# Token-major projections with 512 columns in a matmul instead of 256

## The chip, the core and the metric

The kernel runs on one core of a Trainium2 chip. The metric is the device time of one execution in microseconds (us), the median over several runs. Engines are named as in the profile: PE is TensorE's matmul side and PEld its weight loads, DVE is VectorE, ACT is ScalarE, POOL is GpSimd, SP is the engine that issues the DMAs. PSUM is the memory of eight banks that the matmuls write, each of 512 float32 columns on 128 partitions.

## The reference

Two layers of a streaming-encoder trunk over 512 tokens of 1024 features. Cut to what matters here:

```
y = x @ w_in                       # columns shared by three mixers
  gated linear attention (GLA): value and gate columns, 256 each
  matrix memory (mLSTM): value and output-gate columns, 256 each
  latent attention: two further low-rank projections
x = layer_norm(ALPHA * x + concat(mixers) @ w_out)
x = layer_norm(ALPHA * x + cross_attention(x, mem) @ xa_w_o)
x = layer_norm(ALPHA * x + mixture_of_experts(x))
```

## The kernel before, in words

Every projection multiplies in three float32r matmuls for one product (`mm3`, L383 to L388): high part of the data by high part of the weights, low by high, and high by low. A weight piece is a block of 128 partitions by 1024 columns. `raw_piece` (L356) loads it from SP's queue into one of three buffers ("raw"); `split_raw` (L362) makes the high part on ACT (L350) and the low part on DVE (L351), in three buffers each ("whi", "wlo") or in a page that the caller gives.

Two forms of projection exist. In the feature-major form (`fm_tile`, L390) the weights are the stationary operand and 512 tokens stream. In the token-major form, which the change is about, 128 tokens of the activation are the stationary operand and weight columns stream, so that the result has tokens on its partitions. `tm_weights` (L414) makes two pieces ready, each with four of the eight feature chunks by 256 columns; `tm_tile` (L417) takes one token tile of 128 through all eight chunks, 24 matmuls of 256 columns, into half a bank; `tm_group` (L424) does so for the four token tiles and hands out each result as it is done.

The token-major form is used in four places of each layer:

- `gla` (L850, L852): two groups of 256 columns, the values (copied out by ACT, L851) and the gate (tanh on ACT, L853, and one DVE step, L854);
- `mlstm` (L932, L934): two groups, the values (L933) and the output gate (L935), both evicted by ACT. The four feature-major tiles just before them are evicted by ACT (L922) and three DVE steps each (L925);
- `proj_residual` (L469), called for w_out (L1666) and for the cross-attention's output weights (L1677): four groups of 256 columns. The first two go token tile by token tile; then all pieces of the last two are made ready, the last two of the four on pages, and each token tile takes both groups in turn. A result is added to the residual on DVE (L485) and its statistics taken (L486). Behind a tile's last result comes `finish`: the layer norm on DVE (L457, L458), or in the second call the router, whose first step is a norm on ACT (L1156); then PE transposes the tile (L442).

PSUM has three banks for projections ("pj"), four for everything else ("sm"), and one ("fb") for the projection of the memory tokens, which is put between other work at named places (`filler`) with a fixed number of steps at each. The order of each engine's instructions is fixed when the kernel is built, by a scheduler that goes by program order and by its own estimate of when an instruction can start; on the chip each engine keeps to that order.

Of the kernel before, what the change touches and what calls it, by code (L numbers as in the profile page):

```python
# [13 lines left out]
AF = mybir.ActivationFunctionType  # L14
OP = mybir.AluOpType
# [6 lines left out]
P = 128  # L22
T = 512
NT = 4
D = 1024
KC = 8
# [9 lines left out]
ALPHA = float((2 * L) ** 0.25)  # L36
# [9 lines left out]
PI_GVR, PI_MVO = 12, 16  # L46
PI_UQ, PI_UKV = 20, 22
PI_WO, PI_XQ, PI_XK, PI_XV, PI_XO = 23, 31, 39, 47, 55
# [61 lines left out]
def pack(x, mem, positions, w_in, w_out, gla_w_a2, gla_b_a, gla_norm_g, ml_conv_w, ml_b_i, ml_b_f, ml_norm_g,  # L110
# [4 lines left out]
    x, mem = np.asarray(x)[0], np.asarray(mem)[0]  # L115
# [6 lines left out]
    pieces = np.zeros((L, N_PIECES, P, 1024), f)  # L122
# [6 lines left out]
    def fm(l, i, w):  # L129
        n = w.shape[1] // P  # L130
        for k in range(n):
            pieces[l, i + k] = w[:, k * P:(k + 1) * P].reshape(KC, P, P).transpose(1, 0, 2).reshape(P, -1)

    def tm(l, i, w):
        for g in range(w.shape[1] // 256):
            a = w[:, g * 256:(g + 1) * 256].reshape(2, 4, P, 256).transpose(0, 2, 1, 3).reshape(2, P, 1024)
            pieces[l, i + 2 * g:i + 2 * g + 2] = a

    arr = {k: np.asarray(v) for k, v in dict(
        w_in=w_in, w_out=w_out, uq=mla_w_uq, ukv=mla_w_ukv, xq=xa_w_q, xkv=xa_w_kv, xo=xa_w_o).items()}  # L140
    for l in range(L):
        w = arr["w_in"][l]
        misc = np.zeros((D, P), f)
        misc[:, 0:32], misc[:, 32:36], misc[:, 64:80], misc[:, 96:100] = w[:, kr], w[:, mi], w[:, ga], w[:, mf]
        for i, c in ((PI_CQ, cq), (PI_CKV, ckv), (PI_GQ, gq), (PI_GK, gk), (PI_MQK, mqk)):
            fm(l, i, w[:, c])
        fm(l, PI_MISC, misc)
        tm(l, PI_GVR, np.concatenate([w[:, gv], w[:, gr]], 1))
        tm(l, PI_MVO, np.concatenate([w[:, mv], w[:, mo]], 1))
        u = arr["uq"][l].reshape(256, 8, 96)  # L150
        rp = u[:, :, 64:]
        sw = rp[:, :, (np.arange(32) + 16) % 32]
        u = np.concatenate([u[:, :, :64].reshape(256, 512), rp.reshape(256, 256), sw.reshape(256, 256)], 1)
        pieces[l, PI_UQ], pieces[l, PI_UQ + 1] = u[:P], u[P:]
        kv = arr["ukv"][l].reshape(P, 8, 128)
        pieces[l, PI_UKV] = np.concatenate([kv[:, :, :64].reshape(P, 512), kv[:, :, 64:].reshape(P, 512)], 1)
        tm(l, PI_WO, arr["w_out"][l])
        fm(l, PI_XQ, arr["xq"][l])
        fm(l, PI_XK, arr["xkv"][l][:, :D])
        tm(l, PI_XV, arr["xkv"][l][:, D:])  # L160
        tm(l, PI_XO, arr["xo"][l])

        def col(i, v):
            v = np.asarray(v)[l].reshape(-1)
            n = max(1, v.size // P)
            for k in range(n):
                part = v[k * P:(k + 1) * P]
                cols[l, :part.size, i + k] = part

        col(VC_BA, gla_b_a)  # L170
        col(VC_GG, gla_norm_g)
        col(VC_MG, ml_norm_g)
        col(VC_QG, mla_q_norm_g)
        col(VC_KG, mla_kv_norm_g)
        cw = np.asarray(ml_conv_w)[l].reshape(4, 4, P)
        cols[l, :, VC_CONV:VC_CONV + 16] = cw.transpose(2, 1, 0).reshape(P, 16)
        cols[l, 32:36, VC_MISC] = np.asarray(ml_b_i)[l]
        cols[l, 96:100, VC_MISC] = np.asarray(ml_b_f)[l]
        br[l, 0, 0:4] = np.asarray(moe_b_group)[l]
        br[l, 0, 8:] = np.asarray(moe_b_router)[l]  # L180
        col(VC_LG, ln2_g)
        col(VC_LB, ln2_b)
        for i, v in enumerate((ln1_g, ln1_b, ln2_g, ln2_b, ln3_g, ln3_b)):
            rows[l, i] = np.asarray(v)[l]
        a2[l, 64:80] = np.asarray(gla_w_a2)[l]
        g = np.concatenate([np.asarray(moe_w_group)[l], np.asarray(moe_w_router)[l]], 1)
        g = np.concatenate([g[:, :4], np.zeros((D, 4), f), g[:, 4:]], 1)
        wr[l] = g.reshape(KC, P, NR).transpose(1, 0, 2).reshape(P, -1)
# [20 lines left out]
class K:  # L209
# [202 lines left out]
        return ps  # L412

    def tm_weights(self, i, page=None):  # L414
        return [[v.rearrange("p (k c) -> p k c", k=4) for v in self.piece(i + j, page)] for j in range(2)]

    def tm_tile(self, w, xT, t):  # L417

        ps = self.bank(self.pj)[:, 0:256]
        for k in range(KC):  # L420
            self.mm3(ps, [v[:, k, t * P:(t + 1) * P] for v in xT], [v[:, k % 4, :] for v in w[k // 4]], k == 0, k == KC - 1)
        return ps

    def tm_group(self, i, xT):  # L424

        w = self.tm_weights(i)
        for t in range(NT):
            yield t, self.tm_tile(w, xT, t)

    def new_xT(self):  # L430
        return [self.t([P, KC, T], "T16", 4, F32R, self.tp) for _ in range(2)]
# [37 lines left out]
    def proj_residual(self, l, piece0, srcT, x, ln, xT, page):  # L469

        nc = self.nc
        gb = None if ln is None else self.lnvec(l, ln)
        st = [self.t([P, 4, 6], "ln_st", 4) for _ in range(NT)]
        def finish(t):
            if callable(xT):
                xT(t, st[t], gb)
            else:
                self.layer_norm_tile(x[t], st[t], gb)
                self.x_transpose(x[t], t, xT)

        i = l * N_PIECES + piece0

        def add(g, t, w):
            xs = x[t][:, g * 256:(g + 1) * 256]
            nc.vector.scalar_tensor_tensor(xs, xs, ALPHA, self.tm_tile(w, srcT, t), op0=OP.mult, op1=OP.add)  # L485
            nc.vector.bn_stats(st[t][:, g, :], xs)  # L486

        for g in range(2):
            w = self.tm_weights(i + 2 * g)
            for t in range(NT):  # L490
                add(g, t, w)
        w = [self.tm_weights(i + 4), self.tm_weights(i + 6, page)]
        for t in range(NT):
            for g in range(2):
                add(2 + g, t, w[g])
                if g == 0 and t:
                    finish(t - 1)
        finish(NT - 1)

# [333 lines left out]
    def gla(self, l, xT):  # L833
        nc, v = self.nc, self.vec[l]
        base = l * N_PIECES
        tt = nc.vector.tensor_tensor
        half = lambda z: z.rearrange("p (j t) -> p j t", j=2)
        q, k = half(self.G[0][:, 0, :]), half(self.G[0][:, 1, :])
        nc.scalar.mul(q[:, 0, :], self.gq0, 64 ** -0.5)
        b = self.log_gates(l)  # L840
        for j in range(2):
            if j:
                ps = self.fm_tile(base + PI_GQ + j, xT)
                nc.scalar.mul(q[:, j, :], ps, 64 ** -0.5)
            ps = self.fm_tile(base + PI_GK + j, xT)
            nc.scalar.copy(k[:, j, :], ps)  # L846
        self.fill = self.begin_fill()
        V, gate = self.t([P, 4, 256], "gv"), self.t([P, 4, 256], "gg")

        for t, ps in self.tm_group(base + PI_GVR, xT):  # L850
            nc.scalar.copy(V[:, t, :], ps)  # L851
        for t, ps in self.tm_group(base + PI_GVR + 2, xT):  # L852
            nc.scalar.activation(gate[:, t, :], ps, AF.Tanh, scale=0.5)  # L853
            nc.vector.scalar_tensor_tensor(gate[:, t, :], gate[:, t, :], 1.0, ps, op0=OP.add, op1=OP.mult)  # L854
        ST = [self.t([P, T], f"gS{hh}") for hh in range(2)]
# [12 lines left out]
        n = len(steps)  # L868
# [43 lines left out]
    def mlstm(self, l, xT, mixT):  # L912

        nc, v = self.nc, self.vec[l]
        base = l * N_PIECES
        tt = nc.vector.tensor_tensor
        q, k = self.t([P, 2, T], "mq"), self.t([P, 2, T], "mk")
        for i in range(4):
            ps = self.fm_tile(base + PI_MQK + i, xT)
            y = self.t([P, T], "mconv", 2)  # L920
            w = lambda n: v[:, VC_CONV + 4 * i + n:VC_CONV + 4 * i + n + 1]
# [7 lines left out]
        self.filler("mc")  # L929
        V, gate = self.t([P, 4, 4, 65], "mv"), self.t([P, 4, 256], "mg")  # L930
        nc.vector.memset(V[:, :, :, 64:65], 1.0)
        for t, ps in self.tm_group(base + PI_MVO, xT):  # L932
            nc.scalar.copy(V[:, t, :, 0:64], ps.rearrange("p (h w) -> p h w", h=4))  # L933
        for t, ps in self.tm_group(base + PI_MVO + 2, xT):  # L934
            nc.scalar.activation(gate[:, t, :], ps, AF.Tanh, scale=0.5)  # L935
        Vf = V.rearrange("p c h w -> p c (h w)")

        fc, m, A, A2 = (self.t([4, T], n) for n in ("mfc", "mm", "mA", "mA2"))
# [15 lines left out]
        ps = self.bank()  # L954
# [17 lines left out]
        with self.run_of() as run:  # L972
            for hh in range(2):
                for j in range(2):
                    h = 2 * j + hh
# [4 lines left out]
        for hh in range(2):  # L980
            ps = rows[hh]
            for j in range(2):
                h = 2 * j + hh
# [744 lines left out]
```

## Time and profile before

| | |
|---|---|
| Median of 3 runs | 1617.72 us (1615.04 to 1621.96) |
| The profiled execution's own time | 1623.95 us |
| Its span, first to last instruction | 1622.1 us |
| PE busy | 1555.0 us (96%), 10270 matmuls |
| DVE busy | 1067.8 us (66%) |
| ACT busy | 575.9 us (36%) |
| Mean granted TensorE clock | 0.978 of full speed |

Matmuls are pipelined: the duration in a row runs past the start of the next one, so what a matmul costs in a row of them is the step from start to start. "Idle before" is the time in which the engine had nothing running just before the instruction, with what ended it. A granted clock of 1.00 is 2.4 GHz, one of 0.50 is 1.2 GHz.

### The profile page before, as it was taken

How to read it: one execution, taken by the hardware profiler on the slowest of the kernel's cores; microseconds unless marked ns; L12 is line 12 of the kernel's file. 1: busy time of each engine (PE TensorE's matmuls, PEld its weight loads, DVE VectorE, ACT ScalarE, POOL GpSimd, SP SyncE). 2: the span in 40 equal slices, each digit the busy share in tenths (PEclk: the TensorE clock that was granted, in tenths of full speed). 3: DMA queues.
4: the chain of work that ended last, by engine and by line, in shares of the span. 5: the costliest groups of instructions: out<-in, count | busy, mean ns of one | idle time of the engine just before them, and what ended most of it. 6: DMA issues, size and time to landing. Idle time of an engine off the chain costs nothing. (4 is left out here: it accounts for less than half of the span.)

```text
span 1622.1 us, 25953 instructions
## 1 busy us (share of the span) xinstructions
PE 1555.0 (96%) x10270; PEld 1151.0 (71%) x10270; DVE 1067.8 (66%) x2352; ACT 575.9 (36%) x1026; POOL 32.5 (2%) x44
## 2 busy tenths in 40 slices
PE   7999999999999999999889999999999999999994
PEld 6988876898896555555579888669889855555542
DVE  6768678675568954445767857777655798545454
ACT  6434346324323222222463442552342332222212
POOL 0000000010000000000000000001000000000100
PEclk9999899999999999999999989999999999999997
DMA  6432220522437999996543332033224599899861
GB/s 218 149 119 80 79 72 20 177 68 82 155 121 268 381 341 343 342 352 247 212 152 106 104 98 93 6 122 94 92 86 153 184 351 373 326 339 346 333 238 53
DMA packets 90656, 303.04 MB, mean 187 GB/s; under 512 B 10404, under 2 KB 10916, under 8 KB 90404
## 3 DMA queue, kind: packets, MB, share of 16 engines
q1 hardware_dynamic: 90532, 301.36, 52.7%
q8 instruction: 81, 1.33, 0.3%
q14 instruction: 43, 0.35, 0.1%
HBM read 292.93 MB, written 8.39 MB: 186 GB/s over the span
## 5 line engine op out<-in xcount | busy, mean ns | idle before, releaser
L386 PE MATMUL pj<-whi,T 128*128 128x256 f32 x640 | 183.4, 287 | 4.5 <-ACT T L846 2.8
L1506 DVE TENSOR_TENSOR e<-e,sm 128x512 f32<-128x512 f32 x240 | 153.2, 683 | 51.1 <-PE sm L1502 50.7
L388 PE MATMUL pj<-wlo,T 128*128 128x256 f32 x640 | 182.9, 286 | 3.8 <-DVE wlo L351 3.8
L387 PE MATMUL pj<-whi,T 128*128 128x256 f32 x640 | 182.4, 285 | 0.0
L386 PE MATMUL pj<-T,whi 128*128 128x512 f32 (+1 forms) x368 | 135.3, 368 | 5.9 <-ACT T L350 5.6
L1502 PE MATMUL sm<-e_y,e_oT 128*128 128x512 f32 x512 | 139.3, 397 | 1.3 <-ACT e_y L1385 0.8
L351 DVE TENSOR_TENSOR wlo<-raw,whi 128x1024 fp32r<-128x1024 f32 x86 | 104.7, 1221 | 51.2 <-ACT whi L350 50.7
L387 PE MATMUL pj<-T,wlo 128*128 128x512 f32 (+1 forms) x368 | 135.9, 370 | 2.3 <-DVE wlo L351 2.3
L1320 PEld LDWEIGHTS sm<-oh,T 128*128 128x128 f32 x896 | 117.5, 188 | 25.7 <-issue 17.8
L388 PE MATMUL pj<-T,whi 128*128 128x512 f32 (+1 forms) x368 | 135.0, 368 | 0.0
L1320 PE MATMUL sm<-oh,T 128*128 128x256 f32 x896 | 129.6, 287 | 0.0
L386 PEld LDWEIGHTS pj<-whi,T 128*128 128x128 f32 x640 | 123.9, 194 | 5.8 <-ACT T L846 3.0
L388 PEld LDWEIGHTS pj<-wlo,T 128*128 128x128 f32 x640 | 123.8, 194 | 5.3 <-DVE wlo L351 5.1
L350 ACT CAST whi<-raw 128x1024 fp32r<-128x1024 f32 x86 | 89.8, 1048 | 105.2 <-PE pj L387 57.4
L387 PEld LDWEIGHTS pj<-whi,T 128*128 128x128 f32 x640 | 123.9, 194 | 0.2
L1360 PE MATMUL pj<-e,T 128*64 128x512 f32 x448 | 110.2, 593 | 0.0
L1310 ACT ACTIVATE T<-sm,vec 128x256 f32<-128x256 f32 x116 | 65.3, 566 | 105.1 <-PE sm L1320 105.1
L1502 PEld LDWEIGHTS sm<-e_y,e_oT 128*128 128x128 f32 x512 | 88.1, 188 | 20.4 <-ACT e_y L1385 3.3
L1368 DVE TENSOR_TENSOR e_sl<-e_sl,pj 128x256 f32<-128x256 f32 x32 | 13.5, 421 | 132.7 <-ACT e_sl L1367 132.6
L1385 ACT ACTIVATE e_y<-pj,rws 128x512 fp32r<-128x512 f32 x64 | 43.8, 687 | 118.6 <-PE pj L1383 106.7
L1360 PEld LDWEIGHTS pj<-e,T 128*64 128x64 f32 x448 | 35.1, 137 | 69.9 <-issue 67.7
L386 PEld LDWEIGHTS pj<-T,whi 128*128 128x128 f32 x368 | 70.5, 192 | 17.5 <-ACT T L350 6.4
(483 smaller groups left out, 3200.0 us busy)
## 6 DMA issues: line engine op xcount, KB each, us to landing
e<-in_gu SPq DMA_DIRECT2D x112, 512.0 KB, 9.3
raw<-in_pieces SPq DMA_DIRECT2D x94, 512.0 KB, 3.6
e<-in_dn SPq DMA_DIRECT2D x60, 512.0 KB, 7.6
T<-in_gu SPq DMA_DIRECT2D x44, 512.0 KB, 7.4
wlo<-in_gu SPq DMA_DIRECT2D x36, 512.0 KB, 8.9
whi<-in_gu SPq DMA_DIRECT2D x34, 512.0 KB, 8.8
raw<-in_gu SPq DMA_DIRECT2D x34, 512.0 KB, 8.5
fw<-in_pieces SPq DMA_DIRECT2D x60, 256.0 KB, 3.0
```

What stands on the lines that cost most here:

```text
L350: self.nc.scalar.copy(hi, src)
L351: self.nc.vector.tensor_tensor(lo, src, hi, op=OP.subtract)
L386: mm(ps, a[0], b[0], start=first, stop=False)
L387: mm(ps, a[1], b[0], start=False, stop=False)
L388: return mm(ps, a[0], b[1], start=False, stop=last)
L1310: self.nc.scalar.activation(Xs[:, f, :], ps, AF.Identity, scale=v[:, VC_LG + f:VC_LG + f + 1], bias=v[:, VC_LB + f:VC_LB + f + 1])
L1320: run.append(nc.tensor.matmul(ps, X[i][t][:, f * P:(f + 1) * P], oh[:, t, :], start=i + t == 0, stop=i + t == NT))
L1360: run.append(nc.tensor.matmul(st["h"][CAP * i:CAP * i + CAP, :], Xs[:, k, i * CAP:(i + 1) * CAP], st["w"][i][:, (k % 2) * 512:(k % 2 + 1) ...
L1368: nc.vector.tensor_tensor(sl[0:R], sl[0:R], st["h"][0:R, DE:], op=OP.mult)
L1385: nc.scalar.activation(y[0][0:R, c], po[0:R, :], AF.Copy, scale=ws)
L1502: m = nc.tensor.matmul(ps, ohT[:, t * P:(t + 1) * P], y[i][0:n, c], start=i == 0, stop=i == 1)
L1506: nc.vector.tensor_tensor(x[t][:, c], x[t][:, c], ps, op=OP.add)
```

## The change

A token-major weight piece holds two feature chunks by 512 columns in place of four by 256; the number and size of the pieces stay. `tm_group` takes one result tile of 512 columns for each of the four token tiles at once, in the three "pj" banks and one "sm" bank: a piece is made ready, all four token tiles use it, then the next piece comes. It returns the four results at the end. The groups of `gla` and of `mlstm` that were two are one, with values in the left half of the bank and the gate in the right. In `proj_residual` the first 512 columns go through `tm_group`; for the second 512 the four pieces are made ready and token tile by token tile takes them, the first three tiles in matmuls of 512 columns, the last in two passes of 256. Residual and statistics are done 512 columns at a time, for the last tile's second half 256. The cross-attention's value weights (PI_XV), which are no token-major projection in the kernel, keep the old layout.

```diff
-    def tm(l, i, w):
+    def tm(l, i, w, n=512):
...
     def tm_weights(self, i, page=None):
-        return [[v.rearrange("p (k c) -> p k c", k=4) for v in self.piece(i + j, page)] for j in range(2)]
+        return [v.rearrange("p (k c) -> p k c", k=2) for v in self.piece(i, page)]
 
-    def tm_tile(self, w, xT, t):
+    def tm_tile(self, w, xT, t, c=slice(0, 512)):
 
-        ps = self.bank(self.pj)[:, 0:256]
+        ps = self.bank(self.pj)[:, c]
         for k in range(KC):
-            self.mm3(ps, [v[:, k, t * P:(t + 1) * P] for v in xT], [v[:, k % 4, :] for v in w[k // 4]], k == 0, k == KC - 1)
+            self.mm3(ps, [v[:, k, t * P:(t + 1) * P] for v in xT], [v[:, k % 2, c] for v in w[k // 2]], k == 0, k == KC - 1)
         return ps
 
     def tm_group(self, i, xT):
 
-        w = self.tm_weights(i)
-        for t in range(NT):
-            yield t, self.tm_tile(w, xT, t)
+        ps = [self.bank(self.pj) for _ in range(3)] + [self.bank()]
+        for j in range(4):
+            w = self.tm_weights(i + j)
+            for t in range(NT):
+                for k in (2 * j, 2 * j + 1):
+                    self.mm3(ps[t], [v[:, k, t * P:(t + 1) * P] for v in xT], [v[:, k % 2, :] for v in w], k == 0, k == KC - 1)
+        return ps
...
-        def add(g, t, w):
-            xs = x[t][:, g * 256:(g + 1) * 256]
-            nc.vector.scalar_tensor_tensor(xs, xs, ALPHA, self.tm_tile(w, srcT, t), op0=OP.mult, op1=OP.add)
-            nc.vector.bn_stats(st[t][:, g, :], xs)
-
-        for g in range(2):
-            w = self.tm_weights(i + 2 * g)
-            for t in range(NT):
-                add(g, t, w)
-        w = [self.tm_weights(i + 4), self.tm_weights(i + 6, page)]
+        def add(t, c, ps):
+            xs = x[t][:, c]
+            nc.vector.scalar_tensor_tensor(xs, xs, ALPHA, ps, op0=OP.mult, op1=OP.add)
+            w = 512 if t < NT - 1 else 256
+            for g in range(c.start, c.stop, w):
+                nc.vector.bn_stats(st[t][:, g // w, :], x[t][:, g:g + w])
+
+        for t, ps in enumerate(self.tm_group(i, srcT)):
+            add(t, slice(0, 512), ps)
+        w = [self.tm_weights(i + 4 + j, page if j > 1 else None) for j in range(4)]
         for t in range(NT):
-            for g in range(2):
-                add(2 + g, t, w[g])
-                if g == 0 and t:
+            for c in (0,) if t < NT - 1 else (0, 256):
+                cs = slice(c, c + 512 if t < NT - 1 else c + 256)
+                add(t, slice(512 + cs.start, 512 + cs.stop), self.tm_tile(w, srcT, t, cs))
+                if c == 0 and t:
                     finish(t - 1)
         finish(NT - 1)
...
-        for t, ps in self.tm_group(base + PI_GVR, xT):
-            nc.scalar.copy(V[:, t, :], ps)
-        for t, ps in self.tm_group(base + PI_GVR + 2, xT):
+        for t, ps in enumerate(self.tm_group(base + PI_GVR, xT)):
+            nc.scalar.copy(V[:, t, :], ps[:, 0:256])
+            ps = ps[:, 256:512]
```

## Rows read from the trace of the kernel before

**Rows 1.** The page: span, busy time of three engines, granted clock in 40 slices

```profile
span 1622.1 us, 25953 instructions
PE 1555.0 (96%) x10270; PEld 1151.0 (71%) x10270; DVE 1067.8 (66%) x2352; ACT 575.9 (36%) x1026; POOL 32.5 (2%) x44
...
PEclk9999899999999999999999989999999999999997
```

**Rows 2.** Busy time by stretch (first line: columns): an mLSTM group, both residual projections

```profile
core 0: us, PE busy (x) PEld busy (x) DVE busy (x) ACT busy (x) POOL busy (x), PEclk, DMA share, GB/s
...
143.00:168.00 25.00, 23.96 (x198) 23.45 (x197) 14.94 (x22) 12.11 (x20) 0.00 (x0) 1.00 0.21 64
...
292.00:326.00 34.00, 33.28 (x271) 31.95 (x270) 17.99 (x32) 8.58 (x10) 0.00 (x0) 1.00 0.59 193
...
451.00:482.00 31.00, 29.91 (x240) 27.98 (x238) 19.09 (x83) 9.78 (x12) 1.65 (x3) 1.00 0.22 73
```

**Rows 3.** Groups by line and shape: token-major matmuls; busy, mean ns, idle before, releasers

```profile
L386 PE MATMUL pj<-whi,T 128*128 128x256 f32 x640 | 183.4, 287 | 4.5 <-ACT T L846 2.8 <-ACT whi L350 1.2 <-DVE mconv L925 0.6
L388 PE MATMUL pj<-wlo,T 128*128 128x256 f32 x640 | 182.9, 286 | 3.8 <-DVE wlo L351 3.8
...
L386 PE MATMUL pj<-e,T 128*128 128x256 f32 x64 | 18.9, 295 | 0.0
...
L386 PE MATMUL pj<-wpage,T 128*128 128x256 f32 x64 | 18.5, 289 | 0.0
```

**Rows 4.** PE timeline inside w_out of layer 0: eleven rows, first and last

```profile
302.73 0.28 PE L387 MATMUL pj<-whi,T 128*128 128x256 f32 x1
...
303.93 0.28 PE L388 MATMUL pj<-wlo,T 128*128 128x256 f32 x1
```

**Rows 5.** PE timeline, feature-major tile before mLSTM's groups: thirteen rows, first and last

```profile
139.73 0.39 PE L388 MATMUL pj<-T,whi 128*128 128x512 f32 x1
...
142.45 0.39 PE L388 MATMUL pj<-T,whi 128*128 128x512 f32 x1
```

**Rows 6.** Groups by line and shape: the split of weight pieces on DVE and ACT

```profile
L351 DVE TENSOR_TENSOR wlo<-raw,whi 128x1024 fp32r<-128x1024 f32 x86 | 104.7, 1221 | 51.2 <-ACT whi L350 50.7
...
L350 ACT CAST whi<-raw 128x1024 fp32r<-128x1024 f32 x86 | 89.8, 1048 | 105.2 <-PE pj L387 57.4
```

**Rows 7.** PE timeline at the start of GLA's first group, layer 0

```profile
38.82 0.28 PE L387 MATMUL pj<-whi,T 128*128 128x256 f32 x1
41.87 0.58 PE L386 MATMUL pj<-whi,T 128*128 128x256 f32 x1 [2.77 <-ACT T L846]
...
43.45 0.58 PE L388 MATMUL pj<-wlo,T 128*128 128x256 f32 x1 [0.79 <-DVE wlo L351]
```

**Rows 8.** Busy time of the stretch behind it (columns as in rows 2)

```profile
41.70:48.50 6.80, 5.84 (x25) 5.55 (x26) 6.65 (x8) 1.16 (x2) 0.00 (x0) 0.50 0.64 227
```

**Rows 9.** DVE timeline, layer 0: the last eviction of mLSTM's feature-major tiles

```profile
149.31 1.53 DVE L925 SCALAR_TENSOR_TENSOR mconv<-pj,vec,mconv 128x510 f32<-128x510 f32 x2
```

**Rows 10.** PE timeline, layer 0: mLSTM's first group, its start and its second token tile

```profile
142.68 0.28 PE L386 MATMUL pj<-whi,T 128*128 128x256 f32 x1
...
147.31 0.36 PE L386 MATMUL pj<-whi,T 128*128 128x256 f32 x1 [0.59 <-DVE mconv L925]
```

**Rows 11.** Waits of PE: us in total, times, longest

```profile
PE sm L442 <- ACT e L1156: 2.5, 7, 0.7
PE sm L442 <- DVE e L458: 2.5, 6, 0.4
```

**Rows 12.** DVE timeline, w_out of layer 0: from a tile's last result to its norm

```profile
325.38 0.42 DVE L485 SCALAR_TENSOR_TENSOR e<-e,pj 128x256 f32<-128x256 f32 x1 [1.51 <-PE pj L388]
325.83 0.43 DVE L486 BATCH_NORM_STATS2 ln_st<-e 128x6 f32<-128x256 f32 x1
...
328.38 1.28 DVE L458 SCALAR_TENSOR_TENSOR e<-e,ln_rs,e 128x1024 f32<-128x1024 f32 x1 [0.44 <-POOL ln_rs L451]
```

More of the change, by code (lines that the diff above doesn't have):

```diff
@@ L132, in fm @@
             pieces[l, i + k] = w[:, k * P:(k + 1) * P].reshape(KC, P, P).transpose(1, 0, 2).reshape(P, -1)
-    def tm(l, i, w):
-        for g in range(w.shape[1] // 256):
-            a = w[:, g * 256:(g + 1) * 256].reshape(2, 4, P, 256).transpose(0, 2, 1, 3).reshape(2, P, 1024)
-            pieces[l, i + 2 * g:i + 2 * g + 2] = a
+    def tm(l, i, w, n=512):
+        m = n * KC // 1024
+        for g in range(w.shape[1] // n):
+            a = w[:, g * n:(g + 1) * n].reshape(m, KC // m, P, n).transpose(0, 2, 1, 3).reshape(m, P, 1024)
+            pieces[l, i + m * g:i + m * g + m] = a
     arr = {k: np.asarray(v) for k, v in dict(
@@ L159, in pack @@
         fm(l, PI_XK, arr["xkv"][l][:, :D])
-        tm(l, PI_XV, arr["xkv"][l][:, D:])
+        tm(l, PI_XV, arr["xkv"][l][:, D:], 256)
         tm(l, PI_XO, arr["xo"][l])
@@ L472, in proj_residual @@
         gb = None if ln is None else self.lnvec(l, ln)
-        st = [self.t([P, 4, 6], "ln_st", 4) for _ in range(NT)]
+        st = [self.t([P, 4, 6], "ln_st", 4)[:, 0:2 if t < NT - 1 else 4] for t in range(NT)]
         def finish(t):
@@ L931, in mlstm @@
         nc.vector.memset(V[:, :, :, 64:65], 1.0)
[L932 to L935, printed above, removed]
+        for t, ps in enumerate(self.tm_group(base + PI_MVO, xT)):
+            nc.scalar.copy(V[:, t, :, 0:64], ps[:, 0:256].rearrange("p (h w) -> p h w", h=4))
+            nc.scalar.activation(gate[:, t, :], ps[:, 256:512], AF.Tanh, scale=0.5)
         Vf = V.rearrange("p c h w -> p c (h w)")
```

## The prediction

> **What bounds the kernel now.** I read the page's busy times first, then the busy times by stretch, then the step from one matmul to the next in the PE timeline, and last PE's waits. PE is busy 96% of the span, DVE 66%, ACT 36%, and the granted clock falls below full only in a few slices [rows 1]. A busy PE need not be a bounded one, so the stretches that the change touches are looked at by themselves: in the mLSTM groups of layer 0 PE is busy 23.96 of 25 us with DVE at 14.94, in w_out 33.28 of 34 with DVE at 17.99, in the second half of the cross-attention's output projection 29.91 of 31 with DVE at 19.09 [rows 2]. In all three the sum of matmul steps makes the time, and the other engines have room. So what a matmul costs in a row of them is what counts.
>
> That cost is in the timeline. Ten steps of 256 columns take 303.93 - 302.73 = 1.20 us, 120 ns each [rows 4]. Twelve steps of 512 columns take 142.45 - 139.73 = 2.72 us, 226.7 ns each [rows 5], with the same 128-column weight load ahead of each matmul. Two of 256 cost 240 ns, one of 512 costs 226.7: 13.3 ns are saved for every pair that becomes one. (The durations of 0.28 and 0.39 us in these rows overlap the next matmul and are not used.)
>
> **Wider matmuls.** Each of the three lines of a product has 640 + 64 + 64 = 768 token-major matmuls of 256 columns [rows 3], 384 a layer. After the change a layer has, for each line, 32 of 512 columns in GLA, 32 in mLSTM, and in each of the two residual projections 32 in the first half, 24 for three tiles of the second and 16 of 256 for the last tile: 176 of 512 and 32 of 256. Two layers, three lines: 2 x 3 x 176 x 13.3 ns = **14.0 us less** on PE, 9.0 of it in the residual projections (2 x 2 x 3 x 56 x 13.3 ns = 8.9) and 5.1 in GLA and mLSTM.
>
> By the Trainium skill (TensorE: Matmul & The Clock Gate, section Back-to-back issue gap) a matmul in a row costs its columns at 2.4 GHz plus about 2.5 ns, which would make this term an estimated 2.6 us; the two measured steps here differ from it, and both leave about 13.3 ns above the columns' own time.
>
> **Weight pieces.** Their number, size, loads and splits are the same: 1.05 us on ACT and 1.22 on DVE for each [rows 6], one DMA each, so SP's queue carries the same DMAs. What moves is when a piece is needed. Before, a token tile takes half its 24 matmuls (1.44 us) from the first piece and then needs the second; both stay in use until the last tile, and with three buffers the next pair can't be made ready in full. After, a piece carries 24 matmuls of 226.7 ns, 5.4 us, and frees its buffer then; 5.4 us covers the 2.3 us of a split. All idle time ahead of token-major matmuls sums to 4.5 + 3.8 = 8.3 us, of which 3.8 + 1.2 waited for a split and 2.8 + 0.6 for a bank [rows 3]. The worst place is the start of GLA's first group in layer 0: PE stands from 38.82 to 41.87 and to 43.45 [rows 7], and runs the 6.8 us behind at half clock [rows 8]; there the first piece's high part alone now serves 16 matmuls, 3.6 us, where banks are free. I take **4.0 us less**, the middle between 0 and 8.3.
>
> **Four banks at once.** This is the added wait. A group now wants all three "pj" banks 1.36 us (six matmuls) apart, where it wanted one each 2.88 us. Before mLSTM's group in layer 0 the last feature-major tile still holds its bank until 149.31 + 1.53 = 150.84 [rows 9], 8.2 us behind the group's first matmul at 142.68 [rows 10]; the second tile already waits 0.59 us for the bank before it, to 147.31. Behind a waiting matmul stands all of PE's queue. If the built order has the tiles in turn, PE waits some 2.3 us twice there, 4.6 in place of 0.6; if it puts the fourth tile (in an "sm" bank) and the second piece first, nothing. Bound: 0 to 4.0 us more at this place. The second layer has the same place, so the bound for both is 8.0; I take 1.0 in all, nearer to nothing, since the built orders I see put ready matmuls ahead of ones that wait: in [rows 7] high parts run while the low part is missing.
>
> **Evictions at the end.** In GLA the gate's DVE steps and in both mixers ACT's copies now all come in the last 4 us of a group and just behind it, and what follows (small matmuls that wait for DVE) has them in its queues. Eight ACT and four DVE steps of about 0.4 us; two ACT steps a tile fit the 1.36 us between tiles, so only the last tile's are exposed. Bound: 0 to 1.3 us a group, when the group's own saving is lost in the DVE chain behind it, 5.1 us for all four. I take 1.0.
>
> **Norm and transposes.** In the residual projections' second half PE waits for the norm of a finished tile, 2.5 + 2.5 us over 13 waits [rows 11]. From the last result to the transposes is 325.38 to 329.66, 4.3 us [rows 12]. Residual and statistics of 512 columns each cost up to as much as two of 256, so this chain becomes at most 5.1 us; but between a tile's end and the next tile's end lie 24 x 226.7 ns = 5.44 us, and the transposes are now asked for behind a whole tile and not in its middle. Between 0 and 5.0 us less; I take **1.5 less**, since the router's later waits and the last tile, which keeps its two passes, stay. DVE's fewer, longer evictions are worth nothing: DVE has room.
>
> **Sum.** -14.0 - 4.0 + 1.0 + 1.0 - 1.5 = -17.5 us. The profiled execution took 1623.95 us, 1622.1 of it the span; so 1606.5 for such a run. That execution stood 0.4% above the median of 1617.72; scaled by the same ratio, **1600 us**.
>
> **The rivals.**
>
> *More than that.* All 8.3 us of waits go, the stretch at half clock in GLA goes (25 matmuls [rows 8] of 256 columns at 1.2 GHz, 213 ns in place of 120: 2.3 us), and all 5.0 us of waits for the norm, less 1.0 for the evictions: -14.0 - 8.3 - 2.3 - 5.0 + 1.0 = -28.6, or 1589 us. For it: one late split is the cause of most of them. Against: at the worst place DVE is busy 6.65 of 6.8 us [rows 8] with other work and the low part comes no sooner.
>
> *The gain is swallowed by the mixers.* GLA and mLSTM give back their 5.1 us to the DVE chains behind them, no wait goes, and the bank wait costs 1 to 4 us: -9 + 3 = -6 us, 1612. For it: evictions bunched at the end. Against: DVE stands idle through much of the mLSTM group (14.94 of 25 us [rows 2]), so PE is what the stage waits for.
>
> *Slower, by the banks.* Every group, not only mLSTM's, starts with tiles in turn while banks are still held, and pays 4.6 us of standing PE. It decides from 1.8 us a group (14.0 / 8 groups) on; at 4.6 us a group the sum is 36.8 - 14.0 = 22.8 us slower, **1640 us**, and were each stop followed by half of 6.8 us lost to the clock as in rows 8, another 27 us. Against: only one start shows a bank held for over 3 us [rows 9, 10], and GLA's shows 2.77 us [rows 7] that is already paid.
> The Trainium skill (TensorE: Matmul & The Clock Gate, section HAM oscillation) asks for all feature pieces of an output tile to be run before the next wait for a load, or the clock falls in each wait; the change does the opposite in `tm_group`. Here the order before is the one that the rule asks for, and it is there that rows 7 and 8 show a wait and a clock of 0.50; 5.4 us of matmuls a piece against 2.3 us of split speak against such waits.
>
> *The change does not make the step cheaper.* If the 13.3 ns belonged to the feature-major form alone and a wide token-major step cost 2 x 120 ns, the first term would be 0, the sum -3.5 us, the time 1614. Both steps are of this kernel at full clock with equal weight loads [rows 4, 5], which speaks against it.
> The Trainium skill's rule of about 2.5 ns a matmul (TensorE: Matmul & The Clock Gate, section Back-to-back issue gap) would end beside this rival, at an estimated 1612.
>
> **How the numbers follow.** A measurement of this kernel can tell about 0.5%, 8.1 us, from no change: faster is below 1609.6, slower above 1625.8. The forecast has a chance of 0.55, more than that 0.20, swallowed 0.16, slower by the banks 0.07, no cheaper step, by whatever rule, 0.02. A quarter of the swallowed case lies below 1609.6. Faster 0.55 + 0.20 + 0.04 = 0.79; same 0.12 + 0.02 = 0.14; slower 0.07. The range takes the forecast with its bounds, most of the case above it and the nearer part of the swallowed one: 1590 to 1612.
>
> **What would show it.** Right: PE lines 386 to 388 with 1056 + 192 token-major matmuls in place of 2304, steps of 226.7 ns between those of 512 columns; idle ahead of them below 8.3 us; the w_out stretch shorter by 2.2 us or more; no wait for a split in the middle of a group. The bank term is right if the row of the second or third tile in mLSTM's group waits for L925, and large if it waits over 2 us. Wrong: steps of 240 ns; a granted clock of 0.50 inside a group; new waits of the small matmuls behind GLA's and mLSTM's groups; or the same PE total with the gaps moved into the router's tiles.

## The result and the profile after

The changed kernel takes 1596.4 us (median of four runs, 1593.63 to 1599.63) beside 1616.38 for the kernel before (median of four, 1613.06 to 1621.96). That is a ratio of 0.9874 (95% interval 0.9838 to 0.9909; intervals stand in square brackets below), or 20.0 us less. The forecast was 1600 us, 17.7 less than the median shown then. Run once more beside the experiments, the same kernel took 1594.74 us, a ratio of 0.988 [0.9854, 0.9906].

The page of the changed kernel, to be laid beside [rows 1]:

```profile
span 1591.8 us, 23801 instructions
PE 1530.3 (96%) x9214; PEld 1086.0 (68%) x9214; DVE 1057.7 (66%) x2300; ACT 574.9 (36%) x1026; POOL 32.5 (2%) x44
...
PEclk9999999999999999999999999999999999999997
```

PE has 1056 matmuls fewer than before (x10270), the number of pairs that became one, and is still busy 96% of the span: the bound is the same, and what bounds costs less. The spans of the two profiles differ by 30.3 us, half as much again as the medians. Part of that is the clock; the two answers on the span and mean granted clock of the core, the kernel before first:

```profile
core 0: 1622.1 us, clock 0.978
```

```profile
core 0: 1591.8 us, clock 0.984
```

Span times mean clock gives 1586.4 before and 1566.3 after, 20.1 apart. This product, the span as if at full clock, is used below to compare profiles of different clocks; the last digit of the clock is worth 1.6 us in it, so that the product agrees with the medians to no better than that. It is only a reading, since time in which PE stands doesn't shrink with the clock.

The token-major products in the groups by line and shape of the changed kernel (lines 387 and 389 are what 386 and 388 were), which answer to [rows 3]:

```profile
L387 PE MATMUL pj<-whi,T 128*128 128x512 f32 x240 | 94.9, 395 | 5.5 <-ACT T L853 5.2 <-ACT T L851 0.3
L389 PE MATMUL pj<-wlo,T 128*128 128x512 f32 x240 | 94.0, 394 | 0.9 <-DVE wlo L352 0.9
...
L387 PE MATMUL sm<-whi,T 128*128 128x512 f32 x64 | 25.4, 397 | 0.0
...
L387 PE MATMUL pj<-whi,T 128*128 128x256 f32 x32 | 9.9, 311 | 0.0
...
L387 PE MATMUL pj<-e,T 128*128 128x512 f32 x24 | 9.5, 396 | 0.0
...
L387 PE MATMUL pj<-wpage,T 128*128 128x512 f32 x24 | 9.5, 396 | 0.0
```

240 + 64 + 24 + 24 = 352 wide matmuls on a line. Waits for a split fell from 3.8 + 1.2 us to 0.9; the wait for a bank (L853 is what L846 was) rose from 2.8 to 5.2, and with L851 the idle time ahead of these products went from 8.3 to 6.4.

The step between wide ones, in the PE timeline at w_out of layer 0, answers to [rows 4, 5]; thirteen rows, the first and the last:

```profile
289.76 0.39 PE L388 MATMUL pj<-whi,T 128*128 128x512 f32 x1
...
292.48 0.39 PE L388 MATMUL pj<-whi,T 128*128 128x512 f32 x1
```

Twelve steps in 2.72 us: 226.7 ns, as the feature-major form had it before. The waits for the norm, in PE's waits of the changed kernel, beside [rows 11]:

```profile
PE pj L387 <- ACT T L853: 5.2, 2, 3.3
...
PE sm L447 <- DVE e L463: 0.8, 2, 0.4
```

The 2.5 us for DVE are 0.8, and the 2.5 for ACT's norm in front of the router are not among PE's listed waits any more.

Where it came from, by place: the time from the start of the first to the start of the last token-major matmul of each stretch in the PE timelines, in "pj" and "sm" banks. XO is the cross-attention's output projection; the digit is the layer.

| us | GLA 0 | mLSTM 0 | w_out 0 | XO 0 | GLA 1 | mLSTM 1 | w_out 1 | XO 1 |
|---|---|---|---|---|---|---|---|---|
| before | 29.5 | 25.4 | 54.1 | 61.3 | 26.0 | 24.4 | 53.6 | 61.3 |
| after | 24.9 | 22.5 | 50.1 | 57.9 | 27.3 | 22.9 | 50.1 | 57.9 |

The four residual projections give 14.3 us and the mixers 7.7 in all, although one of their stretches, GLA in layer 1, got longer by 1.4. Of the 4.6 us at GLA of layer 0, up to 3.4 are the clock: the kernel before has the 6.8 us at half clock of [rows 8] there, and this profile none. In GLA of layer 1 the four banks wait. The PE timeline of the changed kernel, GLA of layer 1 (in square brackets the idle time ahead and what ended it):

```profile
827.43 0.50 PE L387 MATMUL pj<-whi,T 128*128 128x512 f32 x1 [0.31 <-ACT T L851]
...
832.37 0.50 PE L387 MATMUL pj<-whi,T 128*128 128x512 f32 x1 [3.28 <-ACT T L853]
...
833.68 0.63 PE L389 MATMUL pj<-wlo,T 128*128 128x512 f32 x1
834.10 0.63 PE L387 MATMUL sm<-whi,T 128*128 128x512 f32 x1
834.53 0.63 PE L388 MATMUL sm<-whi,T 128*128 128x512 f32 x1
```

The third tile stands for 3.28 us until ACT has copied the last feature-major tile out of its bank, and from 833.6 on the steps are 0.43 us, twice 0.2133 (512 columns at 2.4 GHz): the clock is at its lower level, 1.2 GHz. The stretch by itself (columns as in [rows 2]):

```profile
833.60:837.00 3.40, 3.40 (x9) 2.64 (x8) 2.92 (x4) 0.48 (x1) 0.00 (x0) 0.50 0.35 84
```

Why the copy is so late is in the ACT timeline of the changed kernel:

```profile
828.21 1.06 ACT L808 ACTIVATE T<-T 128x1024 f32<-128x1024 f32 x1
...
830.79 1.06 ACT L808 ACTIVATE T<-T 128x1024 f32<-128x1024 f32 x1 [1.52 <-DVE T L806]
831.75 0.57 ACT L853 COPY T<-pj 128x512 f32<-128x512 f32 x1
```

The copy of 0.57 us stands in ACT's queue behind an exp of the gate, which itself waits 1.52 us for DVE. So the bank is held by the order of ACT's queue, not by the copy. Layer 0 has the same wait in a smaller form; the kernel before stood there for 2.77 us [rows 7], and in layer 1 not at all for a bank. The PE timeline of the changed kernel, GLA of layer 0:

```profile
41.77 0.50 PE L387 MATMUL pj<-whi,T 128*128 128x512 f32 x1 [1.87 <-ACT T L853]
```

### The profile page after: what moved, and what is told of

It is laid out like the page before. It is cut to its first block, busy times and chain, and to the rows that moved or that the text cites. A ratio compares the mean times of both kernels' runs of the same rounds, so it can differ in the third digit from the quotient of the medians.

```text
span 1591.8 us, 23801 instructions
## 1 busy us (share of the span) xinstructions
PE 1530.3 (96%) x9214; PEld 1086.0 (68%) x9214; DVE 1057.7 (66%) x2300; ACT 574.9 (36%) x1026; POOL 32.5 (2%) x44
## 5 line engine op out<-in xcount | busy, mean ns | idle before, releaser
L352 DVE TENSOR_TENSOR wlo<-raw,whi 128x1024 fp32r<-128x1024 f32 x86 | 104.7, 1221 | 82.5 <-ACT whi L351 82.1
L387 PE MATMUL pj<-whi,T 128*128 128x512 f32 (+1 forms) x272 | 104.8, 385 | 5.5 <-ACT T L853 5.2
L389 PE MATMUL pj<-wlo,T 128*128 128x512 f32 (+1 forms) x272 | 103.3, 382 | 0.9 <-DVE wlo L352 0.9
L388 PE MATMUL pj<-whi,T 128*128 128x512 f32 (+1 forms) x272 | 103.3, 380 | 0.0
L387 PEld LDWEIGHTS pj<-T,whi 128*128 128x128 f32 x368 | 70.4, 191 | 18.2 <-ACT T L351 7.1
L388 PEld LDWEIGHTS pj<-T,wlo 128*128 128x128 f32 x368 | 70.6, 192 | 13.5 <-DVE wlo L352 2.9
L1372 ACT ACTIVATE e_sl<-pj 128x256 f32<-128x256 f32 x32 | 12.3, 384 | 185.8 <-PE pj L1365 185.8
L389 PEld LDWEIGHTS pj<-T,whi 128*128 128x128 f32 x368 | 70.6, 192 | 11.2 <-issue 1.0
```

What stands on the lines that cost most here:

```text
L352: self.nc.vector.tensor_tensor(lo, src, hi, op=OP.subtract)
L387: mm(ps, a[0], b[0], start=first, stop=False)
L388: mm(ps, a[1], b[0], start=False, stop=False)
L389: return mm(ps, a[0], b[1], start=False, stop=last)
```

## The experiments

My theory after the first result was this: the cheaper step gives most of the gain, fewer waits for splits and for the norm give the rest, and the bank wait in GLA takes some back. There were three rivals: it is the new order of pieces that gains, whatever the width; the mixers' part is lost behind their groups; the wait at GLA costs nothing, since what follows would wait anyway.

### The changed kernel again

There is no edit. The run is the measure for the next three, which ran on the same chip, and shows what two profiles of one kernel have in common. The last three kernels ran on another chip, where the kernel before took 1614.01 us.

> The changed kernel itself, once more, to have its time with a narrower interval beside the others. Both theories: a ratio of 0.986 to 0.990 to the kernel before, some 19 us less; a stretch at half clock may stand in other places than in the first profile.

It took 1594.74 us (six runs), beside 1615.77 for the kernel before (eleven runs): a ratio of 0.988 [0.9854, 0.9906]. Its profile is 1589.3 us at a clock of 0.986, product 1567.0, close to the first one's 1566.3. The token-major stretches agree within 0.1 us in seven of eight places; GLA of layer 0 is 0.9 us longer, with 3.4 us at half clock in it where the first profile has none. The start of mLSTM's group, where the prediction feared for the second tile, in its PE timeline:

```profile
137.79 0.39 PE L387 MATMUL pj<-whi,T 128*128 128x512 f32 x1
...
138.70 1.03 PE L447 MATMUL sm<-const,gg 128*128 128x128 f32 x8
...
140.04 0.40 PE L387 MATMUL sm<-whi,T 128*128 128x512 f32 x1
...
141.43 0.39 PE L387 MATMUL pj<-whi,T 128*128 128x512 f32 x1
```

The tile whose bank is "sm" comes second, a "pj" tile third, and nothing waits.

### The new order with narrow matmuls

The pieces, the order over four banks and the evictions stay; each wide matmul becomes two of 256 columns.

```diff
 def tm_group
-                    self.mm3(ps[t], ..., [v[:, k % 2, :] for v in w], k == 0, k == KC - 1)
+                    for c in (slice(0, 256), slice(256, 512)):
+                        self.mm3(ps[t][:, c], ..., [v[:, k % 2, c] for v in w],
+                                 k == 0 and c.start == 0, k == KC - 1 and c.start > 0)
 def tm_tile
-        ps = self.bank(self.pj)[:, c]
-        for k in range(KC):
-            self.mm3(ps, ..., [v[:, k % 2, c] for v in w[k // 2]], k == 0, k == KC - 1)
-        return ps
+        bank = self.bank(self.pj)
+        for a in range(c.start, c.stop, 256):
+            h = slice(a, a + 256)
+            for k in range(KC):
+                self.mm3(bank[:, h], ..., [v[:, k % 2, h] for v in w[k // 2]], k == 0, k == KC - 1)
+        return bank[:, c]
```

> The changed kernel with its piece layout, four banks and order kept, but each token-major matmul of 512 columns issued as two of 256 into the same bank (1056 more). Theory (the cheaper step gives 14 us, fewer waits the rest): the 14.0 us come back and the rest stays, so 12 to 15 us slower than the changed kernel, ratio 0.994 to 0.998 to the kernel before. Rival (the piece-by-piece order and the later norm give nearly all, the width little): within 4 us of the changed kernel, ratio 0.986 to 0.990.

It took 1604.99 us, a ratio of 0.9932 [0.9914, 0.995], and is 10.2 us above the changed kernel beside it. By the spans it is 14.5 more (1603.8), by span times clock 11.1 (1578.1). Two of these three readings lie below the 12 to 15 us expected. Its PE timeline in w_out of layer 0, nineteen rows, the first and the last:

```profile
289.83 0.28 PE L388 MATMUL pj<-whi,T 128*128 128x256 f32 x1
...
291.99 0.28 PE L388 MATMUL pj<-whi,T 128*128 128x256 f32 x1
```

Eighteen steps in 2.16 us, 120 ns. The eight token-major stretches are 14.7 us longer together than in the changed kernel beside it, of which up to 1.7 are the clock (6.8 us at half clock in GLA of layer 0 beside 3.4). So the width is worth about 10 to 14 us of the 20, against 14.0 by the count of steps, and the rival that puts all of it on the order falls. What is left under the kernel before is 10.8 us by the medians, 8.3 by span times clock and 6.5 by the stretches. It belongs to the order of pieces, the later norm and the other bookkeeping, which this run doesn't part. The opposite edit, wide matmuls token tile by token tile, wants four pieces in memory at a time, and wasn't tried.

### Two banks from each pool

If the wait at GLA and the clock behind it are real losses, a group that takes only two "pj" banks, and two from the "sm" pool, gains. (tm_group takes the number; the projections keep 3.)

```diff
-    def tm_group(self, i, xT):
+    def tm_group(self, i, xT, n=3):
-        ps = [self.bank(self.pj) for _ in range(3)] + [self.bank()]
+        ps = [self.bank(self.pj) for _ in range(n)] + [self.bank() for _ in range(NT - n)]
 GLA and mLSTM
-        ... in enumerate(self.tm_group(base + PI_GVR, xT)):
+        ... in enumerate(self.tm_group(base + PI_GVR, xT, 2)):
-        ... in enumerate(self.tm_group(base + PI_MVO, xT)):
+        ... in enumerate(self.tm_group(base + PI_MVO, xT, 2)):
```

> The changed kernel with two pj and two sm banks in the groups of GLA and mLSTM in place of three and one, so that no group waits for the bank that ACT copies out last (L853). Theory (the four banks cost PE the wait of 5.2 us behind L853 in the two layers, and the half clock behind it in layer 1): the wait for L853 goes and the time falls by 2 to 5 us against the changed kernel. Rival (PE then only waits for the next low part of the weights at the same place): another wait of the same length, the same time within 1.5 us.

It took 1589.59 us, a ratio of 0.9844 [0.9819, 0.9868], 5.2 us below the changed kernel beside it. The span is 1583.0 us at a clock of 0.987, product 1562.4, 4.6 below. The two ratios' intervals overlap a little, so it is the trace that has to show the cause. PE's waits:

```profile
PE pj L389 <- DVE wlo L352: 3.0, 1, 3.0
...
PE pj L387 <- ACT T L851: 0.6, 1, 0.6
```

The 5.2 us for L853 are gone. The group in layer 0 now waits 3.0 us for the low part of its weights, where it waited 0.9 after its wait for a bank: DVE is late there whatever the banks do, and of the 5.2 us some 2 come back. In the first profile of the changed kernel this group took 24.9 us at full clock, and it takes 24.8 here: next to nothing is gained in layer 0. The group in layer 1 gains in full, 22.4 us beside 27.3, and the stretch at half clock behind the wait is gone with the wait. By the medians this is the fastest kernel of the study.

### The second half in two passes again

The norm term alone: the projections' second half as before, 256 columns at a time for every tile, on the new pieces. It takes 2 x 2 x 72 wide matmuls away from the width too.

```diff
 def proj_residual
-        st = [self.t([P, 4, 6], "ln_st", 4)[:, 0:2 if t < NT - 1 else 4] for t in range(NT)]
+        st = [self.t([P, 4, 6], "ln_st", 4) for t in range(NT)]
-            w = 512 if t < NT - 1 else 256
+            w = 256
-            for c in (0,) if t < NT - 1 else (0, 256):
-                cs = slice(c, c + 512 if t < NT - 1 else c + 256)
+            for c in (0, 256):
+                cs = slice(c, c + 256)
```

> The changed kernel with every token tile of the second half of the residual projections in two passes of 256 columns, as only the last tile is in it, with residual and statistics 256 columns at a time. 288 pairs of matmuls come back, 3.8 us. Theory (the waits of the transposes for the norm went because a whole tile now stands ahead of them): PE's waits of L447 for the norm (L463, L1161) come back to 3 us or more, 6 to 9 us slower than the changed kernel. Rival (they went through the widths or by the other changes): they stay below 1.5 us, and the time is 3 to 5 us longer.

It took 1599.09 us, a ratio of 0.9904 [0.9886, 0.9923], 4.4 us above the changed kernel beside it, with intervals that overlap. That is less than the 6 to 9 us expected. PE's waits:

```profile
PE sm L447 <- DVE e L463: 3.0, 8, 0.5
PE sm L447 <- ACT e L1161: 2.8, 8, 0.7
```

5.8 us of waits, where [rows 11] have 5.0 and the changed kernel 0.8. In the PE timeline each of the four projections is longer by 2.1 to 2.2 us (w_out 50.06 to 52.21), 8.7 in all: 288 more matmuls in pairs make 3.8 of it (4 x 72 x 13.3 ns) and the waits 5.0, together 8.8. So the norm term is there, at about 5 us, in the stretches. The whole kernel is only 4.4 us slower, by span times clock as well (1571.4 beside 1567.0). The PE timelines show where a part of the other 4 us went. The way from w_out to the cross-attention's projection is 0.6 us shorter in either layer (73.5 beside 74.2). Between GLA and mLSTM of layer 0, PE waits 1.9 us at the filler for ACT's copy (L1054), beside 3.9; the first profile of the changed kernel has 2.6 there, so this wait changes without any edit. The rest isn't settled.

### Each half of the change by itself

One kernel changes the residual projections and leaves GLA and mLSTM with the old pieces and groups; the other changes GLA and mLSTM and leaves the projections.

```diff
 first kernel
-        tm(l, PI_GVR, ...)
-        tm(l, PI_MVO, ...)
+        tm(l, PI_GVR, ..., 256)
+        tm(l, PI_MVO, ..., 256)
-        for t, ps in enumerate(self.tm_group(base + PI_GVR, xT)):
...
+        for t, ps in self.old_group(base + PI_GVR, xT):
+            nc.scalar.copy(V[:, t, :], ps)
+        for t, ps in self.old_group(base + PI_GVR + 2, xT):
...
 second kernel
-        tm(l, PI_WO, arr["w_out"][l])
-        tm(l, PI_XO, arr["xo"][l])
+        tm(l, PI_WO, arr["w_out"][l], 256)
+        tm(l, PI_XO, arr["xo"][l], 256)
-        for t, ps in enumerate(self.tm_group(i, srcT)):
-            add(t, slice(0, 512), ps)
+        for g in range(2):
+            w = self.old_weights(i + 2 * g)
+            for t in range(NT):
+                add(g, t, w)
...
```

> The change in the residual projections alone; GLA and mLSTM keep two groups of 256 columns from pieces of four chunks. Theory (9.0 us of step and some 5 us of waits for norms and splits lie in the projections): 11 to 16 us less than the kernel before, ratio 0.990 to 0.993, w_out and the cross-attention's projection as short as in the changed kernel. Rival (much of the gain comes from the mixers, whose start and clock change): less than 9 us.

> The change in GLA and mLSTM alone; the residual projections keep 256 columns and their old order. Theory (5.1 us of step, some 2 us of waits, a part of it given back to the evictions at the end of a group): 3 to 8 us less than the kernel before, ratio 0.995 to 0.998, and the stretches behind the groups are as long as before. Rival (the mixers swallow their saving): within 2 us of the kernel before, the stretches behind the groups longer by what the groups are shorter.

The projections alone take 1598.46 us beside 1614.01 for the kernel before, a ratio of 0.99 [0.9884, 0.9916], 15.5 us less. The mixers alone take 1605.75, a ratio of 0.9953 [0.9937, 0.997], 8.3 us less. Together that is 23.8 us beside the 20.0 and 21.0 of the whole change; the product of the two ratios, 0.9853, lies in the first interval of the whole change and just below the second. So the halves add up within what these runs can tell, and the rival that the mixers lose their part behind their groups falls. PE's waits in the kernel with the mixers alone (L861 is the copy out of GLA's last feature-major bank there, L473 and L1169 are the norms):

```profile
PE pj L387 <- ACT T L861: 5.2, 2, 3.3
...
PE sm L457 <- ACT e L1169: 2.7, 8, 0.7
PE sm L457 <- DVE e L473: 2.4, 6, 0.4
```

It has both: the new wait for a bank, and the old waits for the norm. In the kernel with the projections alone the old splits and the old bank wait stand as in [rows 3]; its groups by line and shape:

```profile
L387 PE MATMUL pj<-whi,T 128*128 128x256 f32 x288 | 84.3, 293 | 4.5 <-ACT T L864 2.8 <-ACT whi L351 1.2 <-DVE mconv L942 0.6
...
L389 PE MATMUL pj<-wlo,T 128*128 128x256 f32 x288 | 83.9, 293 | 3.1 <-DVE wlo L352 3.1
```

Each wait thus goes with the half that it was put down to.

The two kernels also show what the late evictions of mLSTM's group hand on. From its last step to the start of w_out in layer 0, the one with the old groups takes 119.4 us and the one with the new 119.8, both with 3.4 us at half clock in it. So at most some 0.4 us are handed back there. From GLA's group in layer 1 to mLSTM's, at full clock in both, they take 64.2 and 63.8 us, and nothing is handed back.

### Two banks from each pool in GLA alone

Of the edit above, only GLA's call.

```diff
-        for t, ps in enumerate(self.tm_group(base + PI_GVR, xT)):
+        for t, ps in enumerate(self.tm_group(base + PI_GVR, xT, 2)):
```

> Two pj and two sm banks in GLA's group alone, mLSTM's with three and one as in the changed kernel. Theory (only GLA's group waits for a bank; mLSTM's built order already goes round it): as fast as the form with two sm banks in both mixers, some 5 us less than the changed kernel. Rival (a part of that gain lies in mLSTM's group): halfway between the two.

It took 1591.07 us, a ratio of 0.9846 [0.9826, 0.9867], beside 0.9844 for the edit in both mixers. PE's waits:

```profile
PE pj L389 <- DVE wlo L352: 3.0, 1, 3.0
...
PE pj L387 <- ACT T L851: 0.3, 1, 0.3
```

What the four banks cost is at GLA's start, where layer 1 takes 22.1 us beside 27.3. In mLSTM there was nothing to gain: its groups take 22.6 and 22.9 us here, 22.5 and 22.9 with two "sm" banks and in the changed kernel.

## Why the prediction was right, point by point

**What bounds.** Right: PE is busy 96% before and after, and what a step saves comes off the end, in each half of the change.

**Wider matmuls, -14.0.** Right in mechanism and count: 3 x 352 wide and 3 x 64 narrow token-major matmuls, 226.7 and 120 ns. The runs at 256 columns give 10.2 us by the medians, 11.1 by span times clock and 14.5 by the spans. The rival without a cheaper step falls: the twelve wide and the eighteen narrow steps of two runs leave 13.3 ns above the columns' own time in both widths. The Trainium skill's formula with about 2.5 ns above the columns (TensorE: Matmul & The Clock Gate, section Back-to-back issue gap) does not agree with that. The section gives it for an isolated matmul, without time for a weight load, and the prediction took it for a row of them; here every matmul has a load of its own (PEld x9214, PE x9214).

**Weight pieces, -4.0.** Half right. The waits for splits fell as the step said, 5.0 to 0.9 us. But the 8.3 us of the bound held 3.4 of waits for a bank, and these did not shrink but grew to 5.5: the sum moved by 1.9, not 4.0. It was wrong to take the middle of a bound made of two kinds of wait, of which the change eases one and aggravates the other.

**Four banks, +1.0.** The mechanism is there, at another place than the step put it. At mLSTM the built order puts the "sm" tile second, as the step hoped. At GLA the rival called layer 0's 2.77 us "already paid", and rightly: that wait is 1.87 now. But the step looked at layer 0 alone, and in layer 1, where the kernel before waited for no bank, the third tile waits 3.28 us. Removing the wait at GLA alone gains 3.7 us by the medians and 5.5 by the ratios (0.988 to 0.9846), with intervals that overlap a little, and 4.9 to 5.2 us in the stretch of layer 1; so the banks cost about 4 to 5 us against a kernel that has none of that wait. Against the kernel before, which waited too, the waits alone are 2.1 more, beside the 1.0 of the step. The rival that ends slower is this mechanism at one start in each layer, not at all eight; its condition, 1.8 us for every group, isn't met.

**Evictions at the end, +1.0.** Hardly seen. The mixers alone gain 8.3 us, more than their 5.1 of steps. Behind mLSTM's group in layer 0, from its last step to w_out's start, 124.1 us became 121.3; the profile before has 6.8 us more of that at half clock, worth up to 3.4, so up to 0.6 may have been handed back. The two kernels with half of the change, at equal clock there, put it at 0.4, and at nothing behind GLA's group in layer 1.

**Norm, -1.5.** Mis-sized. The waits went from 5.0 to 0.8 us, 4.2 less. The step argued that the router's waits for ACT stay; they went with the others, as a whole tile of 24 x 226.7 ns = 5.44 us stands ahead of each transpose. The DVE timeline of the changed kernel in w_out of layer 0 shows the chain, beside [rows 12]:

```profile
317.15 0.69 DVE L491 SCALAR_TENSOR_TENSOR e<-e,pj 128x512 f32<-128x512 f32 x1 [0.80 <-PE pj L389]
317.87 0.69 DVE L494 BATCH_NORM_STATS2 ln_st<-e 128x6 f32<-128x512 f32 x1
318.48 1.27 DVE L352 TENSOR_TENSOR T<-sm,T 128x512 fp32r<-128x512 f32 x2
...
321.70 1.28 DVE L463 SCALAR_TENSOR_TENSOR e<-e,ln_rs,e 128x1024 f32<-128x1024 f32 x1 [0.44 <-POOL ln_rs L456]
323.61 0.69 DVE L491 SCALAR_TENSOR_TENSOR e<-e,pj 128x512 f32<-128x512 f32 x1 [0.63 <-PE pj L389]
```

From 317.15 to 321.70 + 1.28 = 322.98 are 5.8 us, more than the 5.1 bounded: a split of the tile before (L352, two steps, 1.27 us together) stands between statistics and norm. Tile follows tile in 6.46 us (323.61 - 317.15), PE's other work included, and that covers it.

**The sum.** With the measured terms, -14.0 by the steps, -1.9 of waits ahead of the groups and -4.2 at the norm, it is -20.1 us, beside -20.0 by the medians. The forecast of -17.5 took 1.1 us too much for pieces and banks together (-4.0 + 1.0 in place of -1.9), 1.0 too little gain for the evictions and 2.7 too little for the norm. That the sum fits to 0.1 us is partly luck, since the experiments for single terms fit only to 4 or 5 us: the edit of the width moved the medians by 10.2 in place of 14.0, and what it left is 10.8 where the two waits make 6.1.

**More than that, and the clock.** The half-clock stretch of [rows 8], 6.8 us, is gone from GLA of layer 0 in the profile after. In the second profile of the same kernel 3.4 us of it are back, and in the kernel with the mixers alone all 6.8, so it can't be called a gain of the change. By the Trainium skill (TensorE: Matmul & The Clock Gate, section HAM oscillation), which advises it for products of few rows, all feature pieces of an output tile should run before the next wait for a load. No trace here bears that out for 512 tokens: the waits for splits are 5.0 us in that order and 0.9 in the opposite one, and the mean granted clock lies between 0.978 and 0.987 over the executions of the kernel before and between 0.978 and 0.988 over those of the changed one. The wait of 3.28 us and the 3.4 at half clock behind it come from a bank: such a wait with such a stretch stands in all five profiles whose GLA takes three "pj" banks at once, and in neither with two.

## What to carry to other kernels

Where PE is busy nearly all the time, measure the step from one matmul to the next in a timeline at each width: a fixed part of 13 ns a matmul was worth more (14.0 us by the steps) than all the waits that went (6.1). When a loop is turned round so that several banks are open at once, ask for each bank who empties it last and what stands in that engine's queue ahead of it, and split a bound by the kind of wait before taking a middle. A chain of work that has to hide behind a tile hides better when the tile is done in one pass (waits of 0.8 us beside 5.8 here).

## What was not expected of the hardware

Some of the places at half clock move from one execution to the next. The same kernel has 3.4 us at half clock from 75.8 on in its first profile and full clock there in its second, which in turn has 3.4 us from 42.1 on. The two windows in the first and in the second profile (columns as in [rows 2]):

```profile
75.80:79.20 3.40, 3.30 (x15) 3.21 (x15) 3.38 (x6) 2.62 (x5) 0.00 (x0) 0.50 0.48 154
```

```profile
75.80:79.20 3.40, 2.44 (x20) 2.41 (x20) 2.94 (x5) 3.39 (x5) 0.00 (x0) 1.00 0.43 148
42.10:45.50 3.40, 2.93 (x7) 1.83 (x8) 3.40 (x4) 0.00 (x0) 0.00 (x0) 0.51 0.49 171
```

The stretch at GLA of layer 1, behind the wait of 3.28 us, stands in both. A wait for a bank isn't the only thing that it goes with: the kernel with the projections alone has 3.4 us at half clock in that place too, among waits of 1.18 and 1.34 us for a split. The profile before has 10.2 us at half clock behind mLSTM's group in either layer, with PE busy throughout by the profile; in layer 0:

```profile
171.40:181.60 10.20, 10.20 (x102) 7.62 (x101) 4.46 (x9) 2.88 (x5) 0.00 (x0) 0.50 0.42 132
```

Both profiles of the changed kernel have full clock at that place in layer 0. What sets these stretches there isn't shown by any run here. They are why the spans of two profiles should not be subtracted without a look at the clock: 30.3 us between the spans were 20.0 between the medians.
